# Moving GpSimd's elementwise work of a hybrid decoder layer to VectorE and ScalarE, with halos through DRAM and a fourth tile in the weights' ring

## The chip, the cores and the metric

The program runs on one core of a Trainium2 chip. The metric is the device time of one launch in microseconds (us). The core has TensorE (PE in the profile; its weight loads are PEld), VectorE (DVE), ScalarE (ACT), GpSimd (POOL) and SyncE (SP), which here issues nearly all DMAs.

## The reference

One layer of a decoder trunk in fp32, over 2048 prompt tokens (one sequence) and 8 single-token samples that bring their own states:

```python
h = rmsnorm(x, norm_mix);  p = h @ w_in              # 1024 -> 3980 columns
y_a = gated DeltaNet(p_a)   # conv of width 4, chunks of 64: L = exp(g_i - g_j) where i >= j,
                            # M = strict(beta_i * k k^T) * L, triangular solve, state scan
y_b = RWKV-7(p_b)           # token shift xs = p + (prev - p) * mu, low-rank decay, state scan
y_c = HGRN2(p_c)            # gated state, chunks of 64
x = x + concat(y_a, y_b, y_c) @ w_out
h = rmsnorm(x, norm_ffn)
x = x + (silu(h @ w_gate) * (h @ w_up)) @ w_down     # 1024 -> 2816 -> 1024
y = rmsnorm(x, norm_final)                           # and all states are outputs
```

## The kernel before

The tokens are cut in four quarters `q` (512, 512, 512 and 520 columns, the samples at the end of the last); channels lie on the partitions. Every large product is made three times in one-pass fp32 from operands split in two parts, `hi` (rounded) and `lo` (the rest): hi·hi, hi·lo, lo·hi (`mm3`, L359, lines L364 to L366). The splits of activations and weights are elementwise work: ScalarE writes `hi` (L319, L349, L396), and GpSimd or VectorE subtracts for `lo` (L320, L350, L397).

**Weights.** `load_w` (L302) brings a weight tile in halves of 128x512. In the first quarter it loads the raw half into a ring of three (`raw`, L317), splits it (L319 on ACT, L320 on POOL), and stores both parts to DRAM (L327). In the later quarters it loads the split halves from there (L334) into the ring `hl` (L313), which holds three halves in this kernel. Each half serves twelve large matmuls. After the mixing layers are done (`late`), other buffers are used (L332).

**Projection.** For each quarter, 31 tiles of 128 output rows are made (`proj`, L449): VectorE evicts each to a tile `p` (L464) behind three columns of halo, which GpSimd fills from `tail` (L459, or a memset at L457), and GpSimd copies the last three columns back to `tail` (L465). SP stores `p` with its halo to DRAM (L468). The mixers read their slices from there (`slice_p`, L470), the DeltaNet with three columns of halo, RWKV with one.

**Mixers.** A unit is two heads of one group in one quarter, 32 in all; `gdn` (L768), `rwkv` (L963) and `hgrn` (L1150) are generators that yield between steps. Sums over a head's channels go through TensorE (`bsum`, L252): VectorE casts to `hi` (L263), GpSimd makes `lo` (L264), two matmuls add. In `gdn`, the vector `gc` is picked out of the broadcast `g` by a product with the identity (L814) and a reduction (L816); the factor `t` of M is made by two products (L823, L824). In `rwkv`, the token shift is a subtraction on GpSimd (L919) and a fused multiply-add on VectorE (L920). The scans over eight chunks (L859, L1079) alternate small matmuls and small VectorE instructions, each waiting for the other engine.

**The rest.** `out_proj` (L494) and `ffn` (L529) run for one quarter when its mixers are done. A tile of the feed-forward network: VectorE L557, ACT L558 (tanh), VectorE L559 and L560, POOL L561 (product), then the split, ACT L349 and POOL L350.

**Order.** `emit` (L1477) drives it: at each turn every live mixer unit makes one step, and large products are made until their count reaches a due number (`RATES`). The tile scheduler then reorders each engine's stream within the dependences. On the chip each engine runs its own stream in order, waiting for semaphores. SP's stream is in order too: a DMA that waits for a buffer holds up those behind it.

Of the kernel before, what the change touches and what calls it, by code (L numbers as in the profile page):

```python
# [91 lines left out]
class Kern:  # L92
# [209 lines left out]
    def load_w(self, src, key, q, n=1024):  # L302
# [5 lines left out]
        for i in range(n // 512):  # L308
            if self.late:
                hi, lo = (self.T(f"{j}{name}") for j in "hl")  # L310
                parts = hi, lo
            else:
                hl = self.wp.tile([128, 2, 512], F32, tag="hl", name=name)  # L313
                hi, lo = parts = hl[:, 0], hl[:, 1]
            hi, lo = hi.bitcast(F32R), lo.bitcast(F32R)
# [1324 lines left out]
```

## Time and profile before

| | |
|---|---|
| three runs | 3343.81, 3346.0, 3353.82 us (median 3346.0) |
| profiled execution | 3358.87 us, its span 3357.1 us |
| busy in the span | PE 94%, PEld 75%, DVE 63%, ACT 32%, POOL 39% |
| mean granted clock of TensorE | 0.964 of 2.4 GHz |
| DMA | 628 MB in 362,135 packets |

Busy shares are averages over stages that differ. Matmuls are pipelined, so that a busy PE is not a PE at its peak; the start-to-start time of neighbours says more. The first 1100 us are projection beside the mixers of the first quarter and a part of the later ones; to about 1800 us the first `out_proj` and `ffn`, with their weight splits, run beside mixers; then come `ffn` of later quarters beside the last mixers and samples, and from about 2800 us the feed-forward network of the last quarter alone.

### The profile page before, as it was taken

The page shows a single profiled execution, that of the slowest core. Times are in us where ns is not written, and L with a number is a line of the kernel's source. Part 1 is how long each engine was busy: PE and PEld are TensorE (multiplying, and loading weights), DVE is VectorE, ACT ScalarE, POOL GpSimd, SP SyncE. Part 2 cuts the span into 40 slices and gives each one's busy share as a digit, 9 for nine tenths or more (in the row PEclk, how much of TensorE's full clock was granted, in tenths as well). Part 3 has the DMA queues.
Part 4 walks back from the last instruction along what each step waited for, and adds up shares of the span by engine and source line. Part 5 has one row for each costly group of instructions (what it writes and reads, how often), then busy time and mean ns, then how long its engine had stood idle before and what let it go on. Part 6 is the DMA issues. An engine that isn't in the chain of part 4 may idle for free.

```text
span 3357.1 us, 63293 instructions
## 1 busy us (share of the span) xinstructions
PE 3164.3 (94%) x24812; PEld 2520.1 (75%) x24812; DVE 2109.3 (63%) x4577; ACT 1085.6 (32%) x1825; POOL 1325.4 (39%) x1303
## 2 busy tenths in 40 slices
PE   7999999989999999999889999999999999999998
PEld 5766767767888767676656777677767777899998
DVE  6784676587677687767788776666775553332223
ACT  5342232243222445344443333232431222221002
POOL 4752232243222666666573444333331332321113
PEclk9998999999999999999999999999999999999999
DMA  9776656555455756665556345455644447665552
GB/s 301 261 227 206 182 172 202 180 165 178 150 153 169 250 194 215 232 219 198 185 192 184 129 155 169 147 173 168 211 151 155 146 143 249 215 209 184 183 187 92
DMA packets 362135, 628.13 MB, mean 187 GB/s; under 512 B 145580, under 2 KB 150060, under 8 KB 361836
## 3 DMA queue, kind: packets, MB, share of 16 engines
q1 hardware_dynamic: 360748, 623.02, 57.6%
q8 instruction: 195, 3.19, 0.4%
q10 hardware_dynamic: 1088, 1.07, 0.1%
q14 instruction: 104, 0.85, 0.1%
HBM read 456.83 MB, written 167.19 MB: 186 GB/s over the span
## 4 chain that ended last, share of the span: by engine, by line
PE 45%; DVE 11%; DMA 3%; POOL 2%; issue 2%; ACT 1%; SPq 1%; DVEq 0%; POOLq 0%; ACTq 0%
PE pd L364 4%; PE pfu L364 4%; PE pfg L364 4%; PE pfg L366 4%; PE pfg L365 4%; PE pfu L366 4%; PE pfu L365 4%; PE pd L366 4%; PE pd L365 4%; PE pso L364 1%; PE pso L366 1%; PE pso L365 1%; PE pl_h L250 1%; DVE inT_g L656 1%; DVE KV_r L1092 1%
## 5 line engine op out<-in xcount | busy, mean ns | idle before, releaser
L364 PE MATMUL psp<-xs,w_in 128*128 128x512 f32 (+1 forms) x1240 | 457.8, 370 | 32.2 <-DMA w_in<-sw_in 15.4
L366 PE MATMUL psp<-xs,w_in 128*128 128x512 f32 (+1 forms) x1240 | 452.5, 366 | 7.8 <-POOL w_in L320 7.8
L365 PE MATMUL psp<-xs,w_in 128*128 128x512 f32 (+1 forms) x1240 | 452.3, 365 | 0.0
L561 POOL TENSOR_TENSOR t<-t,t 128x512 f32<-128x512 f32 (+1 forms) x110 | 121.6, 1106 | 596.9 <-DVE t L560 583.9
L364 PEld LDWEIGHTS psp<-xs,w_in 128*128 128x128 f32 x1240 | 243.3, 197 | 77.7 <-DMA w_in<-sw_in 18.9
L366 PEld LDWEIGHTS psp<-xs,w_in 128*128 128x128 f32 x1240 | 242.8, 196 | 47.9 <-POOL w_in L320 10.9
L365 PEld LDWEIGHTS psp<-xs,w_in 128*128 128x128 f32 x1240 | 243.1, 196 | 37.2 <-issue 2.0
L579 DVE TENSOR_TENSOR x<-pd,x 128x512 f32<-128x512 f32 (+1 forms) x240 | 137.3, 582 | 146.9 <-PE pd L366 145.5
L364 PE MATMUL pd<-u,w_wd 128*128 128x512 f32 x464 | 194.5, 427 | 19.9 <-DMA w_wd<-sw_wd 7.8
L364 PE MATMUL pfg<-xhs,w_wg 128*128 128x512 f32 x496 | 206.2, 416 | 4.6 <-ACT w_wg L319 3.9
L365 PE MATMUL pfg<-xhs,w_wg 128*128 128x512 f32 x496 | 204.1, 411 | 3.7 <-DVE xhs L537 3.7
L366 PE MATMUL pfg<-xhs,w_wg 128*128 128x512 f32 x496 | 203.9, 411 | 0.2
L364 PE MATMUL pfu<-xhs,w_wu 128*128 128x512 f32 x496 | 201.5, 406 | 0.0
L366 PE MATMUL pfu<-xhs,w_wu 128*128 128x512 f32 x496 | 200.0, 403 | 1.1 <-POOL w_wu L320 1.1
L365 PE MATMUL pfu<-xhs,w_wu 128*128 128x512 f32 x496 | 199.0, 401 | 0.0
L365 PE MATMUL pd<-u,w_wd 128*128 128x512 f32 x464 | 190.3, 411 | 2.1 <-POOL u L350 2.1
L366 PE MATMUL pd<-u,w_wd 128*128 128x512 f32 x464 | 189.0, 409 | 0.2 <-POOL w_wd L320 0.2
L557 DVE TENSOR_TENSOR t<-pfg,rf 128x512 f32<-128x512 f32 (+1 forms) x110 | 64.3, 584 | 175.9 <-PE pfg L366 166.5
L276 ACT ACT_TABLE_LOAD x91 | 116.8, 1283 | 174.8 <-PE kss_r L266 71.2
L558 ACT ACTIVATE t<-t 128x512 f32<-128x512 f32 (+1 forms) x110 | 60.1, 547 | 344.3 <-DVE t L557 340.2
L349 ACT ACTIVATE u<-t 128x512 fp32r<-128x512 f32 (+1 forms) x110 | 60.0, 546 | 304.4 <-POOL t L561 299.0
L560 DVE SCALAR_TENSOR_TENSOR t<-pfu,rf 128x512 f32<-128x512 f32 (+1 forms) x110 | 64.2, 583 | 132.4 <-PE pfu L366 131.6
(645 smaller groups left out, 8469.5 us busy)
## 6 DMA issues: line engine op xcount, KB each, us to landing
w_in<-sw_in SPq DMA_DIRECT2D x186, 512.0 KB, 4.2
w_wg<-sw_wg SPq DMA_DIRECT2D x80, 512.0 KB, 3.2
w_wu<-sw_wu SPq DMA_DIRECT2D x80, 512.0 KB, 3.3
w_wd<-sw_wd SPq DMA_DIRECT2D x72, 512.0 KB, 3.3
sw_in<-w_in SPq DMA_DIRECT2D x62, 512.0 KB, 4.3
s_p<-p SPq DMA_DIRECT2D x93, 257.5 KB, 3.8
sw_wg<-w_wg SPq DMA_DIRECT2D x44, 512.0 KB, 3.7
sw_wu<-w_wu SPq DMA_DIRECT2D x44, 512.0 KB, 3.0
```

The lines of the kernel that those rows point to most:

```text
L250: self.nc.tensor.matmul(out(p), lhsT=lhsT(p), rhs=rhs(p), start=start, stop=stop)
L276: p = self.nc.scalar.preload_act_table_set("natural_log_exp_and_others")
L349: nc.scalar.activation(out[:, 0], src, AF.Copy)
L364: nc.tensor.matmul(ps, lhsT=hi[:, ws], rhs=xs[:, 0, xc], start=start, stop=False)
L365: nc.tensor.matmul(ps, lhsT=hi[:, ws], rhs=xs[:, 1, xc], start=False, stop=False)
L366: nc.tensor.matmul(ps, lhsT=lo[:, ws], rhs=xs[:, 0, xc], start=False, stop=stop)
L557: nc.vector.tensor_tensor(g, psg, r[:, cs], ALU.mult)
L558: nc.scalar.activation(t, g, AF.Tanh, scale=0.5)
L560: nc.vector.scalar_tensor_tensor(p, psu, 0.5, r[:, cs], ALU.mult, ALU.mult)
L561: nc.gpsimd.tensor_tensor(p, p, g, ALU.mult)
L579: nc.vector.tensor_tensor(x2[d][:, c0:c0 + cn], ps, x2[d][:, c0:c0 + cn], ALU.add)
L656: nc.vector.tensor_tensor(tt, U[:, 0:m, m:m + 1].to_broadcast([nb, m, w]), U[:, m:m + 1, m + 1:B].to_broadcast([nb, m, w]), ALU.mult)
```

## The change

All of GpSimd's elementwise instructions but the memsets of `att` and a few of the very last tiles move: most products, sums and `lo` parts to VectorE; the `hi` of `bsum` to ScalarE in return. The token shift becomes a scaled copy on ScalarE, (1-mu)·p, and one fused VectorE instruction. In `gdn` the vector `gc` now comes by a small DMA, transposed, and the factor `t` by one fused instruction (its mask is left to L and to the inverse, which sets the diagonal itself). Halos go through DRAM: the tile `p` has no halo columns; its last three columns are stored into the next quarter's DRAM array by a second DMA, and the first array's halo is zeroed once at the start. The ring `hl` has four halves, `raw` two; `wba` and the `E` tiles are smaller.

```diff
@@ prep_params, dram
+        nc.vector.tensor_scalar(d[:, 16:27], self.parw("mu"), -1.0, 1.0, ALU.mult, ALU.add)
+        self.omu = d[:, 16:27]
...
+        self.nc.vector.memset(zero, 0.0)
+        self.nc.sync.dma_start(self.s_p[0][:, :, 0:HALO].rearrange("m p j -> p m j"),
+                               zero.rearrange("p (m j) -> p m j", j=HALO))
@@ bsum
-            nc.vector.tensor_copy(hi, x)
-            nc.gpsimd.tensor_tensor(lo, x, hi, ALU.subtract)
+            nc.scalar.activation(hi, x, AF.Copy)
+            nc.vector.tensor_tensor(lo, x, hi, ALU.subtract)
@@ load_w
-                hl = self.wp.tile([128, 2, 512], F32, tag="hl", name=name)
+                hl = self.wp.tile([128, 2, 512], F32, tag="hl", name=name, bufs=4)
...
-                raw = self.wp.tile([128, 512], F32, tag="raw", name=f"r{name}", bufs=3)
+                raw = self.wp.tile([128, 512], F32, tag="raw", name=f"r{name}", bufs=2)
...
-                nc.gpsimd.tensor_tensor(lo, raw, hi, ALU.subtract)
+                nc.vector.tensor_tensor(lo, raw, hi, ALU.subtract)
@@ split
-        (nc.vector if by else nc.gpsimd).tensor_tensor(out[:, 1], src, out[:, 0], ALU.subtract)
+        nc.vector.tensor_tensor(out[:, 1], src, out[:, 0], ALU.subtract)
@@ proj
-                nc.gpsimd.tensor_copy(p[:, 0:HALO], self.tail[:, m])
...
-                nc.vector.tensor_tensor(p[:, HALO + c0:HALO + c0 + cn], ps, rstd[q][:, c0:c0 + cn], ALU.mult)
-            nc.gpsimd.tensor_copy(self.tail[:, m], p[:, G:G + HALO])
...
-            nc.sync.dma_start(self.s_p[q][m], p[:, :HALO + n])
+                nc.vector.tensor_tensor(p[:, c0:c0 + cn], ps, rstd[q][:, c0:c0 + cn], ALU.mult)
+
+            if q < 3:
+                nc.sync.dma_start(self.s_p[q + 1][m, :, 0:HALO], p[:, G - HALO:G])
...
+            nc.sync.dma_start(self.s_p[q][m, :, HALO:], p[:, :n])
@@ ffn
-                    nc.gpsimd.tensor_tensor(p, p, g, ALU.mult)
+                    nc.vector.tensor_tensor(p, p, g, ALU.mult)
@@ gdn
+                nc.sync.dma_start(gc[64 * h:64 * h + 64], self.s_g[q][r].rearrange("o (c j) -> j (o c)", j=C))
...
-            nc.gpsimd.tensor_tensor(ch(t), g3, self.bc(self.idS), ALU.mult)
...
-            nc.vector.tensor_reduce(gc, ch(t), AX.X, ALU.add)
...
-            nc.gpsimd.tensor_tensor(ch(t), ch(beB), self.bc(self.nstrict), ALU.mult)
-            nc.gpsimd.tensor_tensor(t, t, L, ALU.mult)
+            nc.vector.scalar_tensor_tensor(t, beB, -1.0, L, ALU.mult, ALU.mult)
@@ shifted
-        nc.gpsimd.tensor_tensor(out, p[:, 0:G], p[:, 1:1 + G], ALU.subtract)
-        nc.vector.scalar_tensor_tensor(out, out, self.par("mu", i), p[:, 1:1 + G], ALU.mult, ALU.add)
+        nc.scalar.activation(out, p[:, 1:1 + G], AF.Copy, scale=self.omu[:, i:i + 1])
+        nc.vector.scalar_tensor_tensor(out, p[:, 0:G], self.par("mu", i), out, ALU.mult, ALU.add)
...
```

The other edits of `gdn`, `rwkv`, `hgrn` and the samples have `nc.vector` in place of `nc.gpsimd` and nothing else. GpSimd's stream shrinks from 1308 instructions to 26; VectorE's grows from 4579 to 5371 (727 more `tensor_tensor` of 512 or so columns, 187 more of 256 or so, 12 more fused ones, 133 casts and 12 reductions fewer); ScalarE's from 1831 to 2075 (169 more activations of 512 columns, 62 tiny ones). TensorE's has the same 19,008.

VectorE's stream in the feed-forward network of the first quarter, from the first instruction of tile 7 (`t_0_7`, `pfg_7`, `pfu_7`), beside mixer instructions (`_r`: RWKV, `_g`: DeltaNet), before:

```order
L557 TENSOR_TENSOR t_0_7_14780<-pfg_7_14729,rf_13158 128x512
L263 CAST hi_bss_r_14857<-t_r_14815 128x512
L1013 TENSOR_TENSOR kr_r_14814<-kr_r_14814,e_r_14652 128x512
L1009 TENSOR_TENSOR kr_r_14814<-kr_r_14814,e_r_14651 128x512
L1084 TENSOR_SCALAR Z_r_14871<-st_r_125,e_r_14648 64x64
L559 SCALAR_TENSOR_TENSOR t_0_7_14780<-t_0_7_14779,t_0_7_14780 128x512
L560 SCALAR_TENSOR_TENSOR t_0_7_14781<-pfu_7_14754,rf_13158 128x512
L920 SCALAR_TENSOR_TENSOR vr_14868<-vr_14868,par_t,pvr_14866 128x512
L871 TENSOR_TENSOR X_g_14979<-px_g_14976,vb_g_13839 128x64
L1020 TENSOR_TENSOR vr_14868<-bss_r_14856,vr_14868 128x512
L1084 TENSOR_SCALAR Z_r_14872<-st_r_125,e_r_14648 64x64
```

GpSimd's stream at the same place before (`rw_wg`, `rw_wu`: raw weight halves; `u_7`: the split tile):

```order
L264 TENSOR_TENSOR lo_bss_r_14858<-t_r_14815,hi_bss_r_14857 128x512
L919 TENSOR_TENSOR vr_14868<-pvr_14866 128x512
L320 TENSOR_TENSOR w_wg_0_14890<-rw_wg_0_14891,w_wg_0_14890 128x512
L320 TENSOR_TENSOR w_wu_0_14897<-rw_wu_0_14898,w_wu_0_14897 128x512
L561 TENSOR_TENSOR t_0_7_14781<-t_0_7_14781,t_0_7_14780 128x512
L320 TENSOR_TENSOR w_wu_0_14904<-rw_wu_0_14905,w_wu_0_14904 128x512
L350 TENSOR_TENSOR u_7_14728<-t_0_7_14781,u_7_14728 128x512
```

VectorE's stream from the same instruction now:

```order
L562 TENSOR_TENSOR t_0_7_14653<-pfg_7_14602,rf_13032 128x512
L959 SCALAR_TENSOR_TENSOR kr_r_14687<-kr_14684,par_t,kr_r_14687 128x512
L961 TENSOR_TENSOR kr_14684<-kr_14684,t_r_14688 128x512
L564 SCALAR_TENSOR_TENSOR t_0_7_14653<-t_0_7_14652,t_0_7_14653 128x512
L962 TENSOR_TENSOR a_r_14568<-kr_r_14687,a_r_14568 128x512
L966 SCALAR_TENSOR_TENSOR t_r_14688<-kr_r_14687,par_t,kr_14684 128x512
L326 TENSOR_TENSOR w_wu_0_14594<-rw_wu_0_14595,w_wu_0_14594 128x512
L682 TENSOR_TENSOR uT_g_14481<-pi_g_14483,cst 128x256
L1015 TENSOR_TENSOR kr_r_14687<-kr_r_14687,e_r_14524 128x512
L1021 TENSOR_TENSOR a_r_14568<-a_r_14568,d_r_14523 128x512
L1019 TENSOR_TENSOR kr_r_14687<-kr_r_14687,e_r_14525 128x512
L1020 TENSOR_TENSOR kr_14684<-kr_14684,d_r_14523 128x512
```

The products (now L961, L962, L1020, L1021, L566), the weights' `lo` (now L326) and `u`'s `lo` (L356) stand between VectorE's own; from the first instruction of tile 7 to that of tile 8 there are 12 others before and 25 now.

SP's stream where the second quarter's projection begins, before (`s_p_146<-p_30` is the last store of the first quarter, `w_in_1` are split weight halves of the second, `raw_x` the next quarter's input):

```order
L468 DMA s_p_146<-p_30_3149 128x515
L384 DMA raw_x_3261<-xT 128x512
L334 DMA w_in_1_3333<-sw_in_0_0_385 128x1024
L384 DMA raw_x_3264<-xT 128x512 x2
L318 DMA rw_o_0_12435<-wo 128x512
L334 DMA w_in_1_3335<-sw_in_0_1_392 128x1024
L334 DMA w_in_1_3440<-sw_in_0_0_429 128x1024
L468 DMA s_p_147<-p_0_3271 128x515
L334 DMA w_in_1_3442<-sw_in_0_1_436 128x1024
```

SP's stream at the same place now:

```order
L469 DMA s_p_148<-p_30_3121 128x3
L473 DMA s_p_147<-p_30_3121 128x512
L390 DMA raw_x_3235<-xT 128x512 x2
L340 DMA w_in_1_3412<-sw_in_0_0_431 128x1024
L478 DMA p_g_3368<-s_p_147 128x515
L340 DMA w_in_1_3414<-sw_in_0_1_438 128x1024
L469 DMA s_p_149<-p_0_3242 128x3
L473 DMA s_p_148<-p_0_3242 128x512
L340 DMA w_in_1_3598<-sw_in_0_0_474 128x1024
L340 DMA w_in_1_3600<-sw_in_0_1_481 128x1024
```

Two weight halves of the second quarter had been issued ahead of the last store of the first before, and four stand ahead of it now; each store of `p` has a store of three columns in front of it.

## Rows read from the trace of the kernel before

**Rows 1.** The page's head and its first part: busy us, share of the span and instructions of each engine.

```profile
span 3357.1 us, 63293 instructions
PE 3164.3 (94%) x24812; PEld 2520.1 (75%) x24812; DVE 2109.3 (63%) x4577; ACT 1085.6 (32%) x1825; POOL 1325.4 (39%) x1303
```

**Rows 2.** Busy time by stage (us from the span's start): stage length, busy us of PE, PEld, DVE, ACT and POOL with their instructions, granted clock, DMA share, GB/s.

```profile
0.00:1100.00 1100.00, 1019.21 (x8760) 798.54 (x8760) 753.87 (x1795) 365.59 (x598) 405.28 (x539) 0.96 0.63 196
1100.00:1800.00 700.00, 640.02 (x4920) 477.44 (x4919) 536.63 (x1035) 315.70 (x537) 448.82 (x340) 0.95 0.64 209
1800.00:2800.00 1000.00, 964.30 (x7058) 726.27 (x7057) 653.87 (x1418) 305.37 (x504) 347.88 (x285) 0.97 0.51 164
2800.00:3357.00 557.00, 540.78 (x4082) 517.87 (x4080) 164.93 (x331) 98.96 (x186) 123.45 (x139) 0.98 0.55 183
```

**Rows 3.** Who ended TensorE's waits, over the span: us in total, times, longest us.

```profile
PE pv_r L250 <- DVE X_r L1090: 17.4, 9, 4.8
PE psp L364 <- DMA w_in<-sw_in: 15.4, 10, 2.7
PE pS_g L881 <- DVE Z_g L877: 8.1, 4, 4.6
PE psp L364 <- ACT xs L396: 8.0, 1, 8.0
PE pd L364 <- DMA w_wd<-sw_wd: 7.8, 3, 3.5
PE psp L366 <- POOL w_in L320: 7.8, 6, 2.3
...
PE ptk_g L712 <- POOL dl_g L851: 3.1, 1, 3.1
...
PE pd L365 <- POOL u L350: 2.1, 3, 1.1
```

**Rows 4.** Busy time by stretch around one wait of TensorE at 793 us, columns as in rows 2.

```profile
793.00:796.00 3.00, 0.79 (x8) 0.48 (x7) 2.96 (x10) 0.38 (x1) 0.19 (x1) 0.92 0.98 335
796.00:802.00 6.00, 5.49 (x14) 3.87 (x16) 3.19 (x9) 0.38 (x1) 0.96 (x2) 0.50 0.25 99
802.00:810.00 8.00, 8.00 (x65) 6.08 (x66) 5.74 (x15) 2.42 (x4) 0.19 (x1) 0.98 0.56 182
```

**Rows 5.** Timeline at 2211 us of SP (one DMA issue, SPq) and of TensorE (two neighbouring large matmuls at the full clock): start, us, line and operands.

```profile
2210.96 0.32 SPq L334 DMA_DIRECT2D w_wg<-sw_wg  x1
...
2211.00 0.40 PE L365 MATMUL pfu<-xhs,w_wu 128*128 128x512 f32 x1
2211.23 0.40 PE L366 MATMUL pfu<-xhs,w_wu 128*128 128x512 f32 x1
```

**Rows 6.** VectorE's costliest groups, shapes apart: count, busy us and mean ns of one, then idle time before.

```profile
L579 DVE TENSOR_TENSOR x<-pd,x 128x512 f32<-128x512 f32 x144 | 97.1, 685 | 64.6 <-PE pd L366 63.2
L1092 DVE SCALAR_TENSOR_TENSOR KV_r<-Z_r,f_r,KV_r 64x64 f32<-64x64 f32 x192 | 84.3, 439 | 4.6 <-ACT KV_r L1069 0.3
...
L797 DVE SCALAR_TENSOR_TENSOR kq_g<-p_g,par_t,kq_g 128x512 f32<-128x512 f32 x72 | 56.1, 805 | 0.5
...
L797 DVE SCALAR_TENSOR_TENSOR cv_g<-p_g,par_t,cv_g 128x512 f32<-128x512 f32 x36 | 40.5, 1124 | 0.7
...
L835 DVE TENSOR_TENSOR Q_g<-pa_g,L_g 64x256 f32<-64x256 f32 x48 | 20.3, 422 | 0.9
...
L1013 DVE TENSOR_TENSOR kr_r<-kr_r,e_r 128x512 f32<-128x512 f32 x12 | 19.9, 1661 | 0.0
...
L816 DVE TENSOR_REDUCE gc_g<-gt_g 128x8 f32<-128x512 f32 x12 | 8.1, 673 | 0.0
```

**Rows 7.** Single lines of VectorE, and one of GpSimd: count, min/median/max ns, first and last start in us.

```profile
L1013 DVE TENSOR_TENSOR kr_r<-kr_r,e_r x12: 678/1769/1780, 139.5 to 2495.2; 128x512 f32<-128x512 f32 x12
...
L797 DVE SCALAR_TENSOR_TENSOR kq_g<-p_g,par_t,kq_g x72: 711/743/1760, 51.4 to 2386.4; 128x512 f32<-128x512 f32 x72
...
L797 DVE SCALAR_TENSOR_TENSOR cv_g<-p_g,par_t,cv_g x36: 731/753/1825, 69.5 to 2407.8; 128x512 f32<-128x512 f32 x36
...
L1092 DVE SCALAR_TENSOR_TENSOR KV_r<-Z_r,f_r,KV_r x192: 257/284/1339, 176.9 to 2757.4; 64x64 f32<-64x64 f32 x192
...
L263 DVE CAST hi_ss_g<-sq_g x24: 408/428/1358, 58.7 to 2403.1; 128x512 fp32r<-128x512 f32 x24
...
L320 POOL TENSOR_TENSOR w_in<-rw_in,w_in x62: 1265/1292/2535, 4.8 to 260.3; 128x512 fp32r<-128x512 f32 x62
```

**Rows 8.** GpSimd's groups, columns as in rows 6.

```profile
L561 POOL TENSOR_TENSOR t<-t,t 128x512 f32<-128x512 f32 x66 | 88.9, 1347 | 331.9 <-DVE t L560 328.4 <-DVE he_h L1214 2.2 <-DVE t L559 1.3
...
L465 POOL COPY tail<-p 128x3 f32<-128x3 f32 x124 | 40.3, 325 | 214.3 <-DVE p L464 208.7 <-DMA w_in<-sw_in 5.2
L264 POOL TENSOR_TENSOR lo_ss_g<-sq_g,hi_ss_g 128x512 fp32r<-128x512 f32 x24 | 35.7, 1487 | 45.8 <-DVE hi_ss_g L263 30.0 <-DMA gB_g<-s_g 14.1 <-PE ss_g L266 1.0
```

**Rows 9.** One group of ScalarE, columns as in rows 6.

```profile
L349 ACT ACTIVATE u<-t 128x512 fp32r<-128x512 f32 x66 | 41.5, 629 | 167.1 <-POOL t L561 161.7 <-PE pd L366 5.1
```

**Rows 10.** DMA issues: count, KB each, median us from issue to landing (`inD<-s_ug` moves runs of 64 bytes).

```profile
w_in<-sw_in SPq DMA_DIRECT2D x186, 512.0 KB, 4.2
...
rw_in<-w SPq DMA_DIRECT2D x62, 256.0 KB, 4.8
...
inD<-s_ug SPq DMA_DIRECT2D x96, 8.0 KB, 1.9
```

More of the change, by code (lines that the diff above doesn't have):

```diff
@@ L29 @@
 HALO = 3
-QW = 523
+QW = 520
 QS = ((0, 512), (512, 512), (1024, 512), (1536, 520))
@@ L344, in stream, with split @@
             yield made[i]
-    def split(self, out, src, by=0):
+    def split(self, out, src):
         nc = self.nc
         nc.scalar.activation(out[:, 0], src, AF.Copy)
-        (nc.vector if by else nc.gpsimd).tensor_tensor(out[:, 1], src, out[:, 0], ALU.subtract)
+        nc.vector.tensor_tensor(out[:, 1], src, out[:, 0], ALU.subtract)
     def cols(self, q):
@@ L424, in stats_x @@
                 j = 32 * (k % 4)
-                nc.tensor.matmul(ps[j:j + 32], lhsT=self.wba[:, k], rhs=load[k][:, cs], start=k < 4, stop=k > 3,
+                nc.tensor.matmul(ps[j:j + 12], lhsT=self.wba[:, k], rhs=load[k][:, cs], start=k < 4, stop=k > 3,
                                  tile_position=(0, j))
-            nc.vector.tensor_copy(p[0:32, cs], ps[0:32])
+            nc.vector.tensor_copy(p[0:12, cs], ps[0:12])
             for j in (32, 64, 96):
-                nc.vector.tensor_tensor(p[0:32, cs], p[0:32, cs], ps[j:j + 32], ALU.add)
-            nc.vector.tensor_tensor(p[0:32, cs], p[0:32, cs], rstd[0:32, cs], ALU.mult)
+                nc.vector.tensor_tensor(p[0:12, cs], p[0:12, cs], ps[j:j + 12], ALU.add)
+            nc.vector.tensor_tensor(p[0:12, cs], p[0:12, cs], rstd[0:12, cs], ALU.mult)
         self.ba(q, p)
@@ L502, in out_proj @@
             nc.sync.dma_start(raw, self.s_mix[q][e])
-            self.split(t[:, :, :n], raw, e % 2)
+            self.split(t[:, :, :n], raw)
             xs.append(t)
@@ L783, in first @@
             g3 = ch(gB)
+            gc = self.sp.tile([128, GC], F32, tag="gc", name=f"gc_{nm}")
+            for h in range(2):
+                r = slice(2 * u + h, 2 * u + h + 1)
+                nc.sync.dma_start(gc[64 * h:64 * h + 64], self.s_g[q][r].rearrange("o (c j) -> j (o c)", j=C))
             sg = self.sp.tile([128, GC], F32, tag="sg", name=f"sg_{nm}")
@@ L843, in first @@
             for h in range(2):
-                (nc.gpsimd if h else nc.vector).tensor_tensor(half(Q, h), q3[H[h]], ch(eg)[H[h]], ALU.mult)
+                nc.vector.tensor_tensor(half(Q, h), q3[H[h]], ch(eg)[H[h]], ALU.mult)
             nc.vector.scalar_tensor_tensor(eg, beB, -1.0, eg, ALU.mult, ALU.mult)
-            nc.gpsimd.tensor_tensor(ch(kb), k3, ch(eg), ALU.mult)
+            nc.vector.tensor_tensor(ch(kb), k3, ch(eg), ALU.mult)
             yield
@@ L1210, in first @@
             for h in range(2):
-                (nc.gpsimd if h else nc.vector).tensor_tensor(half(W, h), ch(q)[H[h]], ch(eb)[H[h]], ALU.mult)
+                nc.vector.tensor_tensor(half(W, h), ch(q)[H[h]], ch(eb)[H[h]], ALU.mult)
                 nc.vector.tensor_copy(half(W, h, True), att[H[h]])
```

50 lines of the change are left out of this document (24 added, 26 removed).

## The prediction

> **What bounds the kernel now.** Read the page's first part first: TensorE is busy 3164.3 of 3357.1 us, so it bounds, and it idles 193 us [rows 1]. Then the stages: the last 557 us run TensorE almost alone, VectorE at 30%; between 1100 and 1800 us VectorE is busy 537 of 700 us and GpSimd 449, and TensorE loses 60 us there against 81 in the first 1100 and 36 in the next 1000 [rows 2]. The reader is to see that TensorE is never far from full, and that what it loses it loses beside a busy VectorE and GpSimd. Then who ends its waits [rows 3]: DMAs of split weights 15.4 + 7.8 = 23 us, GpSimd 7.8 + 3.1 + 2.1 = 13 us, VectorE the rest for the most part, in many small pieces led by the scans (17.4 for X of RWKV, 8.1 for Z of DeltaNet). Taking 8.0 us for the start and some 40 for ScalarE and lesser causes off the 193, I put VectorE's part at 110 us, an estimate from the remainder.
>
> A wait costs more than its length. Around 793 us TensorE idles 2.2 of 3 us and then runs six us at 0.50 of the clock, 1.2 GHz, before it is back at 2.4 GHz [rows 4]. Over the span the clock is 0.96, 0.95, 0.97 and 0.98 by stage [rows 2]: 0.04 x 1100 + 0.05 x 700 + 0.03 x 1000 + 0.02 x 557 = 120 us of full-speed work lost. Idle and clock together are 313 us; what is won of the first brings its share of the second, 120/193 = 0.62 us for each us.
>
> **The change, part by part.**
>
> *Contention that goes.* With one operand in PSUM a 512-column VectorE instruction takes 685 ns (L579). With both in SBUF the same kind has means of 805 and 1124 (L797) and 1661 ns (L1013) [rows 6], while its shortest is 678 (L1013) and its median 743 and 753 (L797) [rows 7]. A 64-column one (L1092) has a median of 284, a mean of 439 and a longest of 1339 ns [rows 6, 7], and 1.3 to 1.5 us is one GpSimd instruction [rows 8]: VectorE stands still for one of GpSimd's. What these groups lose: L797 72 x (805 - 743) and 36 x (1124 - 753) = 18 us, L1092 192 x (439 - 284) = 30, L1013 12 x (1661 - 678) = 12: 60 us on 312 of VectorE's 4577 instructions, 7%. A cast has the same spread (L263 408/428/1358) [rows 7]. I take 300 us for the whole, an estimate, less for each instruction than these lose; its floor is the 60.
>
> *Work that moves to VectorE.* From the streams: 727 instructions of 512 columns at 0.686, 187 of 256 at 0.422 (L835), 12 fused at 0.74: 499 + 79 + 9 = 587 us; less 133 casts at 0.428 = 57 and 12 reductions at 0.673 = 8. Net +522. So VectorE goes from 2109 to 2109 + 522 - 300 = 2331 us, 69% of the span. GpSimd's 1325 us go almost entirely. By stage, with GpSimd's shares in rows 2 as the key (449/1325 = 0.34 for the second): 537 - 102 + 177 = 612 of 700 us, 87%; in the first 754 + 0.31 x 222 = 822 of 1100, 75%; in the third 654 + 0.26 x 222 = 712 of 1000. It fits in every stage, tightly in the second.
>
> *What that does on TensorE's path.* A chain step that was on GpSimd takes 0.69 instead of 1.35 to 1.49 us [rows 8]; one on VectorE loses its contention; in `bsum` the cast and difference (0.43 + 1.49) become 0.63 on ScalarE [rows 9] and 0.69. Against that, between two tiles of the feed-forward network VectorE has 25 instructions where it had 12, and whatever TensorE waits for stands behind them. For the 110 us I bound: -110 if every such wait goes, +55 if queueing makes them half as long again. The two opposite changes of VectorE's load are nearly equal, 522 against 300 plus 1325 us of another engine's; I stay near the middle, -25. For GpSimd's 13 us: half an instruction's length remains, -6 (bounds -13 and +10, where VectorE comes later to a weight's `lo` than GpSimd did).
>
> *The ring.* A half serves twelve matmuls, start to start 0.23 us [rows 5], so 2.8 us. Its reload takes 4.2 us from issue to landing [rows 10] and can't be issued until the old half is read; three halves leave two, 5.6 us, to cover it and SP's queue, four leave 8.4. TensorE's longest waits for them are 2.7 and 3.5 us [rows 3]; one more half covers nearly all. Of the 23 us I take -20 (bounds -23 and 0). In the first quarter `raw` has two instead of three: a raw half lands in 4.8 us [rows 10] and its two splits take 0.63 + 0.69; 62 halves are spread over the first 260 us (L320) [rows 7], 4.2 us each on average, so two cover 8.4 against 6.1 plus VectorE's queue. It holds on average but can fail in bursts: +3, bounds 0 and +25.
>
> *Halos and the rest.* 93 DMAs of three columns and some 24 of `gc` are added, each some 0.32 us of SP's issuing [rows 5]; they land within the 2 us of the other small ones (`inD` 1.9) [rows 10], and are read a quarter later. Cover: SP is not waited for there; without it, 117 x 0.32 = 37 us of issue. VectorE no longer writes `p` behind GpSimd's halo copies, and 0.33 us per `tail` copy (L465) goes with GpSimd [rows 8]: nothing on the path. ScalarE gains 169 x 0.63 = 107 us on 1086, 36% of the span: nothing. The zeros at the start stand ahead of some of the input's loads: +2.
>
> *Sum.* Idle -25 - 6 - 20 + 3 + 2 = -46; the clock's share 0.62 x 46 = -29; and the waits hidden inside busy time, which a modelled end does not show: between 0 and the 46 of the shown ones, I take -20. Together -95 us. The profiled execution took 3358.9 us, 1.8 more than its span and 12.9 more than the median; 3358.9 - 95 = 3264 there, and the median of the runs, 3346.0, becomes 3251. I say 3250.
>
> **The rivals.**
>
> *A. Much more is won.* If lost time and contention are one thing, all waits on VectorE, GpSimd and weights go: (110 + 13 + 23) x 1.62 = 237, so 3110, or with half of VectorE's share left 3200. For it: the long waits follow instructions stretched to 1.3 to 1.8 us. Against: TensorE waits mostly on scans whose steps each cost an exchange with VectorE, which remains. In a sentence beside it, the Trainium skill (SBUF — State Buffer, Who interferes with whom) calls the port pair of the two engines an exclusive lock, by which the loser is blocked for a whole instruction; rows 7 agree (L1092 up to 1339 ns), and by it alone the gain would lie toward 3110.
>
> *B. VectorE's queue takes the place of GpSimd.* Place: 1100 to 1800 us, the first quarter's feed-forward network, where the weights are split too. VectorE now idles 163 us there, chiefly waiting for TensorE. If it must do 612 us of work and keeps those waits, since they are exchanges with TensorE, the stage takes 775, +75; the first stage, with less slack to lose, +30; less the ring's 20 x 1.62 = 32. That is 3346 + 73 = 3419; it decides from the point where VectorE is over 95% busy in the second stage. For it: 25 instructions between two tiles. Against: the contention that goes is most there, and GpSimd's queue too was in order, with weights, products and sums behind one another. The Trainium skill (TensorE: Matmul & The Clock Gate, Architectural detail) says VectorE's queue is strictly first in, first out; no run here shows another behaviour, and by it what was spread over two queues now blocks within one.
>
> *C. Off the path.* The ring's waits move to other buffers, and VectorE's gain and load cancel: 3346, give or take 10. For it: TensorE is 94% busy and has the same 19,008 instructions. Against: rows 3 and 4 show real waits at their price.
>
> **How the numbers follow.** The forecast, 3190 to 3320, has 0.56; A, below that, 0.20; C 0.09; B and milder forms of it 0.15. A measurement of this kernel can tell about 0.3% from no change, 10 us: faster 0.77, same 0.08, slower 0.15, a little of C falling to either side. The range of 8 in 10 reaches into A and into the mild half of B: 3125 to 3370; the likeliest case's own is 3190 to 3320.
>
> **What would show it.** Right: L1013, L797 and L1092 at their medians of before (0.69, 0.75 and 0.28 us as means); VectorE busy 2250 to 2400 us, under 92% between 1100 and 1800 us; TensorE's waits on `sw_in` and `sw_wd` together under 5 us; mean clock above 0.97; TensorE's idle time 130 to 160 us. Wrong: VectorE above 95% in the second stage with TensorE's idle time there above 60 us (B); waits for raw weights of over 25 us (the smaller ring); the same waits of TensorE on VectorE although the long instructions are gone (C).

## The result and the profile after

The changed kernel takes 3230.5 us (median of 4 runs, 3225.3 to 3245.2), the kernel before 3349.9 in the same comparison: a ratio of 0.9652, with a 95% interval of 0.9612 to 0.9692. The forecast was 3250, its range 3125 to 3370. The profiled execution took 3235.6 us, its span 3233.8.

The page's head and first part, after (answers to [rows 1]):

```profile
span 3233.8 us, 62535 instructions
...
PE 3104.7 (96%) x24812; PEld 2475.4 (77%) x24812; DVE 2201.2 (68%) x5369; ACT 1202.5 (37%) x2069; POOL 10.3 (0%) x21
```

TensorE idles 129 us of the span instead of 193, and its mean granted clock is 0.977 instead of 0.964: 0.023 x 3234 = 74 us of full-speed work lost instead of 0.036 x 3357 = 121. So 64 us come from idle time and 47 from the clock, 111 of the span's 123. VectorE has 792 more instructions and is busy only 92 us more.

Busy time by stage, with the boundaries and columns of [rows 2]:

```profile
0.00:1100.00 1100.00, 1022.54 (x8991) 796.42 (x8992) 772.51 (x2015) 428.32 (x751) 2.59 (x10) 0.96 0.67 202
1100.00:1800.00 700.00, 671.01 (x4995) 500.82 (x4995) 572.11 (x1354) 348.32 (x594) 0.53 (x1) 0.97 0.67 217
1800.00:2800.00 1000.00, 993.15 (x7378) 761.91 (x7378) 692.53 (x1628) 361.56 (x587) 2.10 (x4) 0.99 0.55 176
2800.00:3234.00 434.00, 418.05 (x3452) 416.26 (x3450) 164.05 (x376) 64.26 (x138) 5.04 (x6) 0.98 0.54 179
```

Between 1100 and 1800 us TensorE's idle time has halved, 60 to 29 us, though VectorE now does all of GpSimd's work there; it is 82% busy. From 1800 to 2800 us hardly a wait is left (7 us). The first 1100 us are the odd stage: TensorE still idles 77 us.

Who ended TensorE's waits, columns as in [rows 3]:

```profile
PE psp L370 <- ACT w_in L325: 23.8, 9, 7.4
PE psp L370 <- ACT xs L402: 15.2, 4, 7.5
...
PE psp L370 <- DMA w_in<-sw_in: 5.8, 5, 1.9
PE pv_g L881 <- DVE X_g L877: 4.9, 4, 2.0
...
PE px_g L875 <- DVE Z_g L890: 4.0, 3, 2.5
...
PE po_g L897 <- DVE Z_g L883: 2.6, 3, 1.6
...
PE pS_g L887 <- DVE Z_g L883: 0.4, 1, 0.4
```

Waits on VectorE's scan steps (`X`, `Z`) have shrunk, and so have those on reloaded halves `w_in<-sw_in`, 15.4 to 5.8. At the top stands a wait on ScalarE, which writes `hi` of the raw weights (L325).

VectorE's groups that [rows 6] showed:

```profile
L584 DVE TENSOR_TENSOR x<-pd,x 128x512 f32<-128x512 f32 x144 | 97.6, 685 | 47.9 <-PE pd L372 46.7
...
L1098 DVE SCALAR_TENSOR_TENSOR KV_r<-Z_r,f_r,KV_r 64x64 f32<-64x64 f32 x192 | 53.5, 279 | 4.6 <-ACT KV_r L1075 0.8
L806 DVE SCALAR_TENSOR_TENSOR kq_g<-p_g,par_t,kq_g 128x512 f32<-128x512 f32 x72 | 52.0, 741 | 0.4
...
L806 DVE SCALAR_TENSOR_TENSOR cv_g<-p_g,par_t,cv_g 128x512 f32<-128x512 f32 x36 | 26.9, 747 | 0.5
...
L1019 DVE TENSOR_TENSOR kr_r<-kr_r,e_r 128x512 f32<-128x512 f32 x12 | 8.2, 681 | 0.0
```

The group with an operand in PSUM (L584) is where it was, 685 ns. The four with all operands in SBUF went from 439, 805, 1124 and 1661 ns to 279, 741, 747 and 681.

### The profile page after: what moved, and what is told of

Same layout as the page of the kernel before. It is cut to its first block, busy times and chain, and to the rows that moved or that the text cites. A ratio compares the mean times of both kernels' runs of the same rounds, so it can differ in the third digit from the quotient of the medians.

```text
span 3233.8 us, 62535 instructions
## 1 busy us (share of the span) xinstructions
PE 3104.7 (96%) x24812; PEld 2475.4 (77%) x24812; DVE 2201.2 (68%) x5369; ACT 1202.5 (37%) x2069; POOL 10.3 (0%) x21
## 4 chain that ended last, share of the span: by engine, by line
PE 75%; DVE 9%; DMA 8%; ACT 4%; issue 2%; SPq 1%; DVEq 0%; ACTq 0%
PE psp L370 5%; PE pd L370 5%; PE psp L371 5%; PE psp L372 5%; PE pfg L370 5%; PE pfu L370 5%; PE pfu L371 5%; PE pfu L372 5%; PE pfg L372 5%; PE pfg L371 5%; PE pd L372 5%; PE pd L371 5%; DMA rw_in<-w 1%; PE pso L370 1%; PE pso L371 1%
## 5 line engine op out<-in xcount | busy, mean ns | idle before, releaser
L370 PE MATMUL psp<-xs,w_in 128*128 128x512 f32 (+1 forms) x1240 | 449.4, 363 | 44.8 <-ACT w_in L325 23.8
L372 PE MATMUL psp<-xs,w_in 128*128 128x512 f32 (+1 forms) x1240 | 444.5, 359 | 1.2 <-DVE w_in L326 1.0
L371 PE MATMUL psp<-xs,w_in 128*128 128x512 f32 (+1 forms) x1240 | 444.9, 359 | 0.3 <-DVE xs L403 0.3
L370 PEld LDWEIGHTS psp<-xs,w_in 128*128 128x128 f32 x1240 | 235.9, 190 | 94.4 <-ACT w_in L325 29.0
L372 PEld LDWEIGHTS psp<-xs,w_in 128*128 128x128 f32 x1240 | 235.6, 190 | 40.2 <-DVE w_in L326 4.9
L371 PEld LDWEIGHTS psp<-xs,w_in 128*128 128x128 f32 x1240 | 236.2, 191 | 36.2 <-DVE xs L403 2.7
L584 DVE TENSOR_TENSOR x<-pd,x 128x512 f32<-128x512 f32 (+1 forms) x240 | 138.2, 582 | 116.0 <-PE pd L372 114.5
L371 PE MATMUL pfg<-xhs,w_wg 128*128 128x512 f32 x496 | 199.2, 402 | 5.7 <-DVE xhs L542 5.5
L370 PE MATMUL pfg<-xhs,w_wg 128*128 128x512 f32 x496 | 201.6, 406 | 1.1 <-ACT w_wg L325 1.1
L372 PE MATMUL pfg<-xhs,w_wg 128*128 128x512 f32 x496 | 198.3, 400 | 0.0
L370 PE MATMUL pd<-u,w_wd 128*128 128x512 f32 x464 | 189.5, 416 | 2.6 <-DVE x L584 2.2
L371 PE MATMUL pd<-u,w_wd 128*128 128x512 f32 x464 | 188.0, 405 | 0.1
L372 PE MATMUL pd<-u,w_wd 128*128 128x512 f32 x464 | 186.6, 403 | 0.0
L355 ACT ACTIVATE u<-t 128x512 fp32r<-128x512 f32 (+1 forms) x110 | 59.9, 545 | 212.9 <-DVE t L566 211.8
L466 DVE TENSOR_TENSOR p<-psp,ri 128x512 f32<-128x512 f32 (+1 forms) x155 | 90.0, 581 | 52.9 <-PE psp L372 49.4
```

The lines of the kernel that those rows point to most:

```text
L355: nc.scalar.activation(out[:, 0], src, AF.Copy)
L370: nc.tensor.matmul(ps, lhsT=hi[:, ws], rhs=xs[:, 0, xc], start=start, stop=False)
L371: nc.tensor.matmul(ps, lhsT=hi[:, ws], rhs=xs[:, 1, xc], start=False, stop=False)
L372: nc.tensor.matmul(ps, lhsT=lo[:, ws], rhs=xs[:, 0, xc], start=False, stop=stop)
L466: nc.vector.tensor_tensor(p[:, c0:c0 + cn], ps, rstd[q][:, c0:c0 + cn], ALU.mult)
L584: nc.vector.tensor_tensor(x2[d][:, c0:c0 + cn], ps, x2[d][:, c0:c0 + cn], ALU.add)
```

## The experiments

All times are medians of 4 executions or more, compared with the kernel before on the same chip, which took 3346.8 to 3349.9 us in the four comparisons. The first run is a base for others: room in SBUF for a scratch tile, or for a third raw half, had to come from somewhere.

One thing limits most of these prices. The tile scheduler orders the engines' streams anew for each kernel. In e2 and b3, with the added instructions left out, TensorE, VectorE and ScalarE run in the base's order but for a few neighbours (b3's 24,812 matmuls stand in the same places, e2's all but 54). In the other runs, c_A28 included, the order differs from that of the kernel they are compared with, from one of the first thousand or so matmuls on. What a new order alone is worth was not measured, so prices of some 10 to 75 us from these runs hold for the edit together with its order.

**c_A28**, one temporary tile of the mixers fewer.

```diff
-LANES = {"A": (29, 2, "A"), ...
+LANES = {"A": (28, 2, "A"), ...
```

> The changed kernel with 28 instead of 29 temporary tiles in lane A of the mixers: the base of the next three runs, which need the 2 KB per partition. Both theories: the changed kernel's time, 3230 us, within 12 us, and VectorE busy 2201 us as there.

Measured: 3236.7 us (3235.5 to 3238.1), 6 above the changed kernel's median and inside the spread of its runs. Its page's first part:

```profile
PE 3109.9 (96%) x24812; PEld 2478.0 (77%) x24812; DVE 2199.4 (68%) x5369; ACT 1199.2 (37%) x2065; POOL 10.2 (0%) x21
```

**e2_pool_noise**, GpSimd made busy again with work that nobody needs.

```diff
+        self.scr = self.cp.tile([128, G], F32, name="scr")
@@ proj, after the evictions of a tile p: noise(p, 5); ffn, after the product p: noise(p, 3)
+    def noise(self, x, k):
+        self.nc.gpsimd.tensor_copy(self.scr[:, 0:3], x[:, 0:3])
+        for _ in range(k):
+            self.nc.gpsimd.tensor_tensor(self.scr, self.scr, self.scr, ALU.subtract)
```

> The base with added GpSimd instructions that nothing waits for: five of 512 columns on a scratch tile of its own after each projected tile, three after each tile of the feed-forward network (950 instructions of some 1.3 us, 1235 us), paced by a copy of three columns of the tile. Nothing is taken away, and the outputs are the same. Theory 1 (contention): the two engines hinder each other wherever both work in SBUF, so that VectorE's shortest and mean times part again (the 64-column multiply-add of the RWKV scan from a mean of 0.28 back to 0.37 us or more), VectorE is busy 2201 + 250 to 350 us, and since VectorE's steps lie on TensorE's path the time rises by 60 to 120 us. Theory 2 (what counted was GpSimd's own place on the path, as a slow step that others waited for): VectorE's times may stretch, but the time rises by less than 25 us.

Measured: 3434.3 us (3429.1 to 3441.9), 198 above its base and slower than the kernel before. The page's first part, three groups of VectorE, the scan step's shortest, median and longest ns, and four of TensorE's waits:

```profile
PE 3164.3 (92%) x24812; PEld 2511.3 (73%) x24812; DVE 2619.8 (76%) x5369; ACT 1198.8 (35%) x2065; POOL 1199.6 (35%) x1206
```

```profile
L595 DVE TENSOR_TENSOR x<-pd,x 128x512 f32<-128x512 f32 x144 | 97.2, 683 | 34.1 <-PE pd L381 33.3
L1109 DVE SCALAR_TENSOR_TENSOR KV_r<-Z_r,f_r,KV_r 64x64 f32<-64x64 f32 x192 | 93.4, 487 | 3.7
...
L817 DVE SCALAR_TENSOR_TENSOR cv_g<-p_g,par_t,cv_g 128x512 f32<-128x512 f32 x36 | 33.9, 942 | 0.3
...
L1109 DVE SCALAR_TENSOR_TENSOR KV_r<-Z_r,f_r,KV_r x192: 264/285/1128, 214.4 to 2833.4; 64x64 f32<-64x64 f32 x192
```

```profile
PE pv_g L892 <- DVE X_g L888: 21.0, 12, 3.4
...
PE px_g L886 <- DVE Z_g L901: 12.2, 10, 2.3
...
PE pS_g L898 <- DVE Z_g L894: 10.1, 10, 2.3
...
PE po_g L908 <- DVE Z_g L894: 8.3, 7, 3.9
```

The same 5369 VectorE instructions are busy 420 us longer (2619.8 against 2199.4). The 64-column step of the RWKV scan has a mean of 487 ns again, and TensorE's waits on the DeltaNet's `X` and `Z` add up to 52 us where the changed kernel has 12. The group with PSUM keeps its 683 ns. No engine waits for the added instructions for more than 2 us in all, so it is not the tiles they read that hold the others up. Theory 1 holds, above its numbers: a us of stretched VectorE cost 198/420 = 0.47 us. That is a mean: where TensorE had streamed 30% of its matmul columns the run was 147 us late with VectorE 260 us busier (0.57), and the rest brought 44 us for 160 (0.28).

**e3_dve_noise**, the same with VectorE (two and three instructions, no copy). Without the copy nothing ties the added instructions to the tiles they were written behind, and the scheduler put all of them early.

> The base with VectorE instructions that nothing waits for: two of 512 columns on a scratch tile after each projected tile, three after each tile of the feed-forward network (578 instructions of 0.68 us, 393 us). It prices a us of added VectorE work, of which the change brought 522 by my sum. Theory 1 (a us of VectorE is worth the same whether it comes from contention or from work): 393 us cost about as much for each us as contention does, 80 to 130 us in all. Theory 2 (VectorE has room, and only steps that stand on a chain count): under 30 us. Rival B of the prediction would show as VectorE over 92% busy beside TensorE's first feed-forward network, with a steeper price there.

Measured: 3304.7 us (3298.1 to 3306.2), 68 above its base. The page's first part, and the added group twice (the second line has the shortest, median and longest ns and the first and last start in us):

```profile
PE 3127.9 (95%) x24812; PEld 2492.1 (75%) x24812; DVE 2530.3 (77%) x5948; ACT 1180.6 (36%) x2053; POOL 10.2 (0%) x21
```

```profile
L222 DVE TENSOR_TENSOR scr<-scr 128x512 f32<-128x512 f32 x578 | 394.5, 683 | 4.7
...
L222 DVE TENSOR_TENSOR scr<-scr x578: 627/683/696, 2.6 to 1029.2; 128x512 f32<-128x512 f32 x193
```

578 instructions of 683 ns are 395 us, but busy time rises by 331, since neighbours overlap. For the whole run that is 68/331 = 0.21 us for each us of busy time. But all 578 ran before 1030 us, beside the projection and none beside a feed-forward network. Busy time by stretch, columns as in [rows 2], the base and then this run:

```profile
0.00:1100.00 1100.00, 1025.41 (x8994) 796.68 (x8995) 769.36 (x2004) 420.71 (x742) 2.07 (x9) 0.96 0.66 202
1800.00:2800.00 1000.00, 995.52 (x7274) 763.73 (x7274) 686.21 (x1615) 359.49 (x583) 2.11 (x4) 1.00 0.55 175
```

```profile
0.00:1100.00 1100.00, 990.86 (x7988) 775.45 (x7988) 999.41 (x2290) 355.70 (x636) 2.06 (x9) 0.93 0.64 195
1800.00:2800.00 1000.00, 975.54 (x7795) 739.71 (x7794) 747.37 (x1862) 391.54 (x660) 2.10 (x4) 0.99 0.52 166
```

TensorE idles 35 us more in the first stretch, where the work was added, and 20 more in the other, where none was. Where it had streamed 30% of its matmul columns the run was 38 us late, at 60% 34, and the rest of the 68 came behind that, where nothing but the order of the streams differs. So the added work cost between about 40/331 = 0.12 and 0.21 us for each us. Both theories fall: work is not free, and it was less than half as dear as stretched instructions. What it costs beside a feed-forward network was not measured.

**b3_memset_noise**, e2 with writes alone.

```diff
-            self.nc.gpsimd.tensor_tensor(self.scr, self.scr, self.scr, ALU.subtract)
+            self.nc.gpsimd.memset(self.scr, 0.0)
```

> e2_pool_noise (3434 us; its base 3237) with its 950 GpSimd subtractions replaced by 950 memsets of the same scratch tile, which write SBUF and read nothing (some 0.53 us each, 500 us together). Theory 1 (an instruction of GpSimd's holds VectorE off for its whole length whatever it does in SBUF): VectorE is stretched in proportion to GpSimd's busy time, by about 170 us, and the time rises by about 80 us to 3300 to 3340. Theory 2 (it is the two reading operands that VectorE is held off by): VectorE within 20 us of its 2199 us and the time under 3250.

Measured: 3242.2 us (3238.9 to 3242.9), 5 above the base. The page's first part, and the scan step (count, shortest, median and longest ns):

```profile
PE 3102.0 (96%) x24812; PEld 2474.6 (76%) x24812; DVE 2209.1 (68%) x5369; ACT 1199.3 (37%) x2065; POOL 581.2 (18%) x1206
```

```profile
L1109 DVE SCALAR_TENSOR_TENSOR KV_r<-Z_r,f_r,KV_r x192: 256/281/289, 186.6 to 2644.0; 64x64 f32<-64x64 f32 x192
```

GpSimd is busy 581 us, and VectorE 2209 with a longest scan step of 289 ns. Theory 2 holds: memsets don't hinder VectorE, instructions that read two operands in SBUF do. An instruction with one operand was not tried by itself.

**e9_ffn_pool**, GpSimd keeps its part of the weights and of the feed-forward network.

```diff
-nc.vector.tensor_tensor(lo, raw, hi, ALU.subtract)
-nc.vector.tensor_tensor(p, p, g, ALU.mult)
-nc.vector.tensor_tensor(out[:, 1], src, out[:, 0], ALU.subtract)
+nc.gpsimd. ... (in load_w, ffn and split)
```

> The changed kernel with the weights' lo, the feed-forward product and the activations' lo on GpSimd (some 550 instructions of 512 or 256 columns), all mixer work staying on VectorE. By the prices of the two noise runs (0.47 us of time for a us of stretched VectorE, 0.17 for a us of work): GpSimd busy some 640 us, VectorE stretched by some 215 us for +100 us, and 310 us less work for -53: 3265 to 3295 us. Rival B of the prediction (VectorE's queue is what holds TensorE beside the first feed-forward network): faster than the changed kernel, under 3220 us.

Measured: 3304.8 us (3299.1 to 3308.7), 74 above the changed kernel: 10 above the range that the two prices gave, and far from what rival B asks for. The page's first part and one of ScalarE's waits:

```profile
PE 3126.8 (95%) x24812; PEld 2486.6 (75%) x24812; DVE 2101.4 (64%) x4907; ACT 1202.3 (36%) x2070; POOL 599.2 (18%) x483
```

```profile
ACT u L355 <- POOL t L566: 236.1, 79, 7.2
```

GpSimd's product stands ahead of `hi` again, and 79 times ScalarE waits for it, 236 us in all. Little of that comes from GpSimd, though; in the changed kernel ScalarE waits nearly as long for VectorE's product. The kernel before, then the changed one:

```profile
ACT u L349 <- POOL t L561: 299.0, 87, 10.1
```

```profile
ACT u L355 <- DVE t L566: 211.8, 75, 8.4
```

TensorE idles 60 us between 1100 and 1800 us, as in the kernel before; in the changed kernel it is 29. VectorE got rid of 462 instructions, worth an estimated 245 us of busy time (331/578 = 0.57 us each by e3, less for the shorter ones), yet is busy only 100 us less, so about 145 are stretch. By the prices 145 x 0.47 - 245 x 0.21 = +17, and measured are 74: an estimate of 57 us is left (35 with 0.12 for the added work). GpSimd's steps being twice as long on the way of a tile is one explanation, the new order of the streams another; no run parts them.

**x_raw3A28**, three raw halves.

```diff
-tag="raw", name=f"r{name}", bufs=2)
+tag="raw", name=f"r{name}", bufs=3)
```

> The base with three raw weight tiles in the first quarter instead of two, the ring of split halves at four as in the changed kernel. Theory 1 (the smaller raw ring is what made the first 300 us worse: TensorE idles 55 us there, where it idled 35 before): TensorE's waits for w_in in the first 300 us fall from 24 to under 10 us, and the time by 15 to 30 us against the base. Theory 2 (those waits come from the start, the zeros written ahead of the loads and VectorE being later to the weights): less than 8 us.

Measured: 3202.5 us (3200.0 to 3204.1), 34 below its base. TensorE's waits in the first 300 us, the base first, then this run:

```profile
PE psp L370 <- ACT w_in L325: 22.2, 8, 6.7
```

```profile
PE psp L370 <- ACT w_in L325: 12.1, 8, 5.3
```

The time moved as theory 1 said, a little beyond it; the wait halved rather than falling under 10. How a raw half is held shows in SP's waits of the first 300 us, the changed kernel and then this run:

```profile
SPq L333 <- DVE w_in L326: 41.8, 19, 16.6
```

```profile
SPq L333 <- DVE w_in L326: 18.6, 15, 3.2
```

A store of split weights stands in SP's queue until VectorE has made `lo`, up to 16.6 us with two raw halves and 3.2 with three, and the raw loads stand behind it. With two halves the next raw load needs the same `lo` for its buffer, so that whether the store or the ring holds it back can't be told apart here. Over the whole span TensorE's direct waits on raw weights fell from 33.0 us in the base to 13.5; with the 0.62 to 0.73 us of clock that went with each us of idle time, an estimate of 32 to 34 us, which is the time won.

**e1_ring3**, both rings as before the change.

```diff
-tag="hl", name=name, bufs=4)     tag="raw", ..., bufs=2)
+tag="hl", name=name, bufs=3)     tag="raw", ..., bufs=3)
```

> The changed kernel with both rings as before: three split halves, three raw halves. With x_raw3A28 (four and three, 3202 us) it prices the fourth split half, with the changed kernel (four and two, 3230 us) the whole edit of the rings. Theory 1 (the prediction's term: the fourth half takes TensorE's waits on reloaded weights away, 20 us and their share of the clock): 3225 to 3240 us, with 10 to 25 us of waits of TensorE on sw_in and sw_wd, so that the edit of the rings as a whole was worth nothing. Theory 2 (the fourth half is idle once GpSimd is out of the way): 3195 to 3210 us.

Measured: 3230.9 us (3227.3 to 3232.3): theory 1. TensorE's waits on reloaded weights:

```profile
PE psp L370 <- DMA w_in<-sw_in: 12.3, 13, 4.4
...
PE pd L370 <- DMA w_wd<-sw_wd: 3.5, 4, 1.2
```

15.8 us. The fourth half is worth 3230.9 - 3202.5 = 28 us, the third raw half 34. The first of these compares 29 temporary tiles with 28; with the tile's 6 us it would be 34 too. The edit of both rings was worth nothing (3230.9 against 3230.5, with runs of the changed kernel from 3225 to 3245).

**e7_halo_before**, the halos' part alone, in the kernel before.

```diff
-nc.gpsimd.tensor_copy(p[:, 0:HALO], self.tail[:, m])   (and the memset and the copy to tail)
+nc.sync.dma_start(self.s_p[q + 1][m, :, 0:HALO], p[:, G - HALO:G])
...
+zeros to s_p[0] at the start
```

> The kernel before (3348 us) with one part of the change alone: halos through DRAM, the zeros stored at the start. GpSimd keeps the rest of its work. The prediction's term: +2 us, nothing on the path, so 3340 to 3360 us. Rival 1 (117 more issues on SP's queue and small pieces cost): 15 to 40 us slower. Rival 2 (VectorE's evictions had waited behind GpSimd's halo copies): 10 to 20 us faster.

Measured: 3366.6 us (3362.4 to 3376.7) against 3346.8, ratio 1.0059 (1.0038 to 1.0080): 20 us slower, rival 1's low end. Busy time of the first 300 us, columns as in [rows 2], the kernel before and then this run:

```profile
0.00:300.00 300.00, 264.54 (x1616) 194.73 (x1617) 199.46 (x389) 120.99 (x199) 157.70 (x183) 0.94 0.80 260
```

```profile
0.00:300.00 300.00, 241.77 (x1482) 172.97 (x1483) 198.38 (x373) 114.89 (x191) 139.23 (x109) 0.89 0.75 224
```

TensorE has 23 us less work done by 300 us. How much of that is the zeros, the small stores or the new order, this run does not show.

**e5_zero_late**, x_raw3A28 with the four lines on `zero` moved from `dram` to `load_consts`, behind the first projected tile.

> x_raw3A28 (3202 us) with the zeros for the first halo stored after the first projected tile, with the other constants, not ahead of the input's loads. Theory 1 (the 3968 pieces of 12 bytes hold up the input: TensorE's first 50 us have 9 us less work than before the change, and its waits for the first xs are 15 us against 8): 6 to 14 us faster. Theory 2 (the start is late for another reason, VectorE or the raw ring): within 4 us.

Measured: 3190.8 us (3188.6 to 3192.8), 12 less. SP's timeline at the start (start, us of issuing), the changed kernel and then this run:

```profile
2.13 0.91 SPq L390 DMA_DIRECT2D raw_x<-xT  x2
3.37 0.39 SPq L205 DMA_DIRECT2D s_p<-zero  x1
3.80 7.01 SPq L390 DMA_DIRECT2D raw_x<-xT  x2
```

```profile
2.12 3.05 SPq L391 DMA_DIRECT2D raw_x<-xT  x6
```

Two loads of `raw_x` behind the zeros take 7.01 us to issue; without the zeros ahead of them six take 3.05. Theory 1. This is the fastest kernel of the study, ratio 0.9531 (0.9502 to 0.9560).

**b2_raw4, b1_halo_act, b4_E4**: three more steps from e5. The first two needed room and took it from the mixers' tiles, 27 of them.

```diff
@@ b2_raw4
+tag="raw", ..., bufs=4        LANES = {"A": (27, ...
@@ b1_halo_act
+nc.scalar.activation(p[:, 0:HALO], self.tail[:, m], AF.Copy)     (no small stores, no zeros; 27)
@@ b4_E4
+pool(name="ev", bufs=4)       LANES = {"A": (29, ...
```

> e5_zero_late (3191 us) with four raw weight halves, one temporary tile of the mixers fewer for the room. Going from two to three was worth 34 us. Theory 1 (bursts still empty the ring of three: TensorE waits 12 us for w_in in the first 300 us): 3178 to 3188 us. Theory 2 (three halves cover the load, the waits left are the start): within 5 us.

> e5_zero_late (3191 us) with the halos kept in SBUF, copied from and to the tail by ScalarE (tiny activations, three columns each; the zeros of the first quarter by VectorE), so that no small store and no zeros go to DRAM; one temporary tile fewer for the room. e7_halo_before cost 20 us and the zeros at the start were 12 of them, so theory 1 (the rest, 8 us, is the 93 small stores on SP's queue): 3178 to 3188 us. Theory 2 (the rest was GpSimd's order, and ScalarE's copies ahead of each eviction add a wait): 3191 to 3205 us.

> e5_zero_late (3191 us) with the room for the third raw half taken from the eviction tiles (four instead of five) and the mixers' 29 temporary tiles kept. The base run put the 29th tile at 6 us. Theory 1 (an eviction tile is free again within a store's 4 us, so four do): 3182 to 3190 us. Theory 2 (in the feed-forward network three eviction tiles go to each product, so four hold it up): 3195 to 3230 us.

Measured: 3236.1, 3230.8 and 3217.7 us; all three slower than e5. Busy time of the first 300 us and of 1800 to 2800 us, columns as in [rows 2]: e5, b2, b1.

```profile
0.00:300.00 300.00, 262.64 (x1621) 191.80 (x1621) 205.57 (x474) 129.27 (x213) 1.01 (x7) 0.93 0.86 262
1800.00:2800.00 1000.00, 986.68 (x7398) 764.42 (x7397) 685.82 (x1618) 346.25 (x577) 2.10 (x4) 0.99 0.55 179
```

```profile
0.00:300.00 300.00, 270.97 (x1640) 204.71 (x1640) 200.75 (x450) 121.50 (x203) 1.01 (x7) 0.95 0.88 276
1800.00:2800.00 1000.00, 960.33 (x7440) 731.85 (x7441) 711.87 (x1736) 368.41 (x614) 2.10 (x4) 0.97 0.51 164
```

```profile
0.00:300.00 300.00, 278.70 (x1736) 209.42 (x1736) 206.46 (x502) 134.89 (x260) 1.01 (x7) 0.99 0.87 283
1800.00:2800.00 1000.00, 937.99 (x7259) 718.60 (x7258) 704.20 (x1723) 359.20 (x604) 2.10 (x4) 0.95 0.50 158
```

b2 and b1 met neither of their theories. Both gain in the first stretch (TensorE 271 and 279 us against 263), as their first theories have it, and lose in the other (960 and 938 against 987), where no raw half is loaded. What the two have in common is the 27 tiles; no run changed them alone, and e3, with 28, loses 20 us in the same stretch by its order. So the cause of this loss stays open. b1's 279 us is the best start of all, above the 264.5 of the kernel before. For b4 the time is theory 2's: the fifth eviction tile, with its order, is worth 27 us more than the 29th temporary one; that the feed-forward network is what it holds up was not looked at.

## Why the prediction was right, step by step

The time lies 20 us below the forecast. The direction and the main cause were as forecast; that the sum came so near is in part luck, because terms that were off had both signs.

- **Idle time and clock.** Forecast -46 and -29, and 20 more hidden in busy time; measured, on the spans, -64, -47 and 12 more. Each us of idle time brought 0.73 of clock, not 0.62.
- **Contention that goes.** Confirmed by the groups and by e2. At e3's 331 of 395 the forecast's 522 us of work are 438 of busy time; VectorE rose by 92, so that 346 us of stretch went, an estimate, where 300 were taken. The traces agree: the 4279 VectorE instructions that both kernels have under the same names and shapes last 2040 us in sum before and 1715 after, 325 less. Its 2201 us fall under the forecast's 2250 to 2400.
- **What that does on TensorE's path.** This is the step that failed in size: "The two opposite changes of VectorE's load are nearly equal ...; I stay near the middle, -25". It priced a us of stretch like a us of work. By e2 and e3 they are 0.47 and 0.12 to 0.21: an estimate of 346 x 0.47 = 163 us won and 53 to 92 of 438 lost, -110 to -71 together, clock included, where -25 x 1.62 = -40 stood. The waits of e2 suggest why: a stretch falls on any instruction that has its operands in SBUF, the scans' small ones too, for which TensorE waits each time. Why added work costs less is not shown.
- **GpSimd's steps.** Forecast -6. Rings 0 (e1), halos +20 (e7) and the -71 make -51; of the measured -119 some 68 are left, and with -110 only 29. e9 has 35 to 57 by subtraction for its 462 instructions. Both are remainders of estimates and hold whatever a new order of the streams brings, so that GpSimd's steps were worth more than the 6 us is argued, not shown. The forecast took TensorE's 13 us of direct waits on GpSimd as the measure. There is a way over ScalarE too, whose wait for the product went from 299.0 us (161.7 of them for the 512-column tiles [rows 9]) to 211.8; whether TensorE gains by that no run shows.
- **The ring.** The fourth half: -20 of idle time, with the clock -32; measured -28. The smaller `raw`: +3 of idle time, with the clock +5, bounds 0 and +40; measured +34. The step that failed is "two cover 8.4 against 6.1 plus VectorE's queue. It holds on average": VectorE's queue was given no size, and SP waited for its `lo` up to 16.6 us at a time, with the next raw load behind the waiting store.
- **Halos and the rest.** Forecast nothing and +2; measured +20 in the kernel before. The zeros were 12 in e5's kernel; the other 8 stay open, as b1 met neither theory. The issue price of 0.32 us [rows 5] is not that of a load behind 3968 pieces of 12 bytes, 3.5 us.
- **The rivals.** B is out: VectorE is 82% busy in its stage, TensorE idles 29 us there, and to give VectorE's queue relief (e9) costs 74 us. C is out by the time, and so is A with 3110, or 3200 in its milder form. A's mechanism, that lost time and contention are one thing, is right in part, with 0.47 for a price; but it holds for GpSimd instructions that read from SBUF, not for every one (b3). The Trainium skill (SBUF — State Buffer, Who interferes with whom) states the lock for a VectorE instruction with two inputs in SBUF only against a GpSimd instruction that reads SBUF. e2 (1128 ns) and b3 (289 ns) agree with that, and L584's 685 ns with one operand in PSUM too.
- **The marks.** Means of 0.68, 0.75 and 0.28 us: met. VectorE under 92% in the second stage, clock above 0.97: met. Waits on reloaded halves under 5 us: 5.8. Idle time of 130 to 160 us: 129. Of the signs of being wrong one came, though the forecast held: TensorE's waits for raw weights, over 25 us, were 28.6 (23.8 in the row above, the rest in smaller ones).

## What to carry to other kernels

A us of an engine is not one price: ask whether the time sits on steps that another engine waits for, and measure it with work that nobody needs, once on each engine. Then look in the trace where that work ran and whether the rest kept its order: e2's did, e3's did not. An elementwise instruction taken from GpSimd pays by VectorE's instructions in SBUF that it no longer stretches, and perhaps by its own length. When a change brings several parts, look for the ones that lose: here the smaller raw ring and the zeros ahead of the input's loads took back 46 us against a base with one tile fewer, and with both undone the kernel is at 0.953 instead of 0.965.

## What was not expected of the hardware

- GpSimd's memsets of 128x512, 530 ns each, left VectorE as it was (a longest scan step of 289 ns), while subtractions with two operands in SBUF stretched it to 1128 ns.
- VectorE's busy time rose by 331 us for 578 instructions of 683 ns: 16% of their time lay beside that of neighbours.
- One strided store of 12-byte pieces made the next two loads take 7.0 us to issue on SP, against 0.5 us each.
